# Element-wise two-tensor operations of more than 300 elements on VectorE alone, small ones also on GpSimd, in a two-layer attention encoder

## The chip, the cores and the metric

One core of a Trainium2 chip runs the whole program. The metric is device time in microseconds of one execution: the median of several runs, and beside it the time of one profiled execution, on which the trace is made. Engines are named as in the profile: PE (matrix products), DVE (VectorE), ACT (ScalarE), POOL (GpSimd), SP (issues DMA).

## What is computed

Two sequences, of 1024 and of 512 positions, go through the same two encoder layers; 16 learned positions are put ahead of each, so that the kernel works on 1040 + 528 = 1568 columns of width 1024. Everything is in 32-bit floats. Cut to what matters:

```python
def layer(x, cos, sin, w_in, w_out, pre_g, post_g, sink, lq1, lk1, lq2, lk2, subln_g, lambda_init):
    h = rmsnorm(x, pre_g)
    aq, ak, av, ag, bq, bk, bv, bg = split(einsum('bld,de->ble', h, w_in))
    aq, ak = apply_rope(aq, cos, sin), apply_rope(ak, cos, sin)
    oa = window_gqa_attention(aq, ak, av, sink) * silu(ag)      # 8 heads, a window of 128 on either side
    lam = exp(sum(lq1 * lk1)) - exp(sum(lq2 * lk2)) + lambda_init
    bq, bk = apply_rope(bq, cos, sin), apply_rope(bk, cos, sin)
    ob = diff_attention(bq, bk, bv, lam, lambda_init, subln_g) * silu(bg)   # softmax(c=0) - lam * softmax(c=1)
    o = einsum('ble,ed->bld', concatenate([oa, ob]), w_out)
    return x + rmsnorm(o, post_g)
```

## The kernel before

Features lie on the partitions, positions along the free dimension. The 1568 columns are worked on in four chunks of 392 (`CH`). For each layer the program has these steps: `prestats` and `rstd_bc` sum the squares of a chunk and broadcast the reciprocal root `rb` of it; `prenorm` scales the chunk; `load_w` brings weights; `inproj` and `project` multiply and make queries, keys, values and gates (with rope), which are stored to HBM; `attn_b` (four heads of the differential kind) and `attn_a` (two groups of the windowed kind) read them back; `outproj` multiplies by `w_out`, and its `post` normalises, adds the residual and stores.

A product is made in two parts for precision: every operand is split into a rounded part `hi` and the rest `lo = x - hi`, and three products are summed in PSUM (`dense`: hi by hi, hi by lo, lo by hi). So each weight tile (`whl`, 128x1024), each normalised chunk (`slot`), each rope result (`st`) and each probability tile (`at`) needs a copy and then a subtraction. `dense` writes its sums to `ps_d`, which has two buffers; `ps_s` holds scores, `ps_t` transposes, `ps_o` attention outputs.

Nothing is issued in the order of the code. `Recorder` notes each operation with what it reads and writes, its priority, and a cost for each engine that can do it (`Engine.form`, lines 460 to 522). `schedule` (line 323) then runs through time by these costs and hands the next ready operation of highest priority to an engine that is free; an operation that has two engines goes to whichever can take it first. What comes out is one fixed order for each engine, which `emit` issues (line 445, the line that all instructions carry in the profile). Each engine then works its own queue in that order and waits at its head.

Operations with two engines come from three helpers: `any_copy` (ACT or DVE), the squares of `prestats` in the first layer (ACT or POOL, line 722), and `any_tt` (line 296, DVE or POOL), which is called for all two-tensor additions, subtractions and products whose inputs both lie in SBUF:

```python
            cost = 0.15 + n * (0.0022 if name == "tensor_tensor" else 0.0035)   # POOL, line 512
                cost = 0.066 + n * 0.001042                                      # DVE, line 508
```

`n` is the number of elements per partition. Both forms also carry a mark `port`; by it the planner lets no two of them overlap in time (lines 398 to 408).

Names of tiles: `t` (in the code `t1`) holds the first half of a rope product or the running sum of squares of an output chunk; `ru` and `rw` are rope products or squares; `sm` small columns (minima, sums, reciprocal roots); `pp` probabilities; `og` attention output; `pad` the last 16 keys. In `rstd_bc` POOL always does two short operations on `sm` (TENSOR_SCALAR, and a power with `mhalf`), between two transposes of PE.

Of the kernel before, what the change touches and what calls it, by code (L numbers as in the profile page):

```python
# [125 lines left out]
ENG = ("PE", "ACT", "DVE", "POOL", "SP")  # L126
PE_COL = 0.0004453
PE_SWITCH = 0.39


def _size(pat, shape, kw):
# [106 lines left out]
class Recorder:  # L238
# [55 lines left out]
        return self.call([g[0] for g in got], got[0][1], got[0][2])  # L294

    def any_tt(self, out, a, b, op):
        return self.any((self.vector, "tensor_tensor", (out, a, b), dict(op=op)),
                        (self.gpsimd, "tensor_tensor", (out, a, b), dict(op=op)))

# [158 lines left out]
class Engine:  # L458
# [3 lines left out]
    def form(self, name, args, kw):  # L462
# [14 lines left out]
        elif self.eng == "PE":  # L477
# [10 lines left out]
            if src.shape[0] <= 64:  # L488
                cost += PE_SWITCH
        elif self.eng == "ACT":  # L490
# [1027 lines left out]
```

## Time and profile before

| | before |
|---|---|
| median of 3 runs (lowest, highest) | 1985.34 us (1983.41, 1994.87) |
| the profiled execution | 1988.96 us |
| its span from the first to the last instruction | 1986.8 us |
| mean granted clock of PE | 0.972 |
| busy: PE, DVE, ACT, POOL | 1841.9, 1509.0, 1015.0, 825.2 us |

The profiled execution is 0.2% above the median. The span leaves 2.2 us of it outside. A stretch in which PE is busy throughout is at PE's pace, whatever the other engines do; the waits of PE in the other stretches say whose result ended last.

### The profile page before, as it was taken

The page shows a single profiled execution, that of the slowest core. Times are in us where ns is not written, and L with a number is a line of the kernel's source. Part 1 is how long each engine was busy: PE and PEld are TensorE (multiplying, and loading weights), DVE is VectorE, ACT ScalarE, POOL GpSimd, SP SyncE. Part 2 cuts the span into 40 slices and gives each one's busy share as a digit, 9 for nine tenths or more (in the row PEclk, how much of TensorE's full clock was granted, in tenths as well). Part 3 has the DMA queues.
Part 4 walks back from the last instruction along what each step waited for, and adds up shares of the span by engine and source line. Part 5 has one row for each costly group of instructions (what it writes and reads, how often), then busy time and mean ns, then how long its engine had stood idle before and what let it go on. Part 6 is the DMA issues. An engine that isn't in the chain of part 4 may idle for free. (4 is left out here: it accounts for less than half of the span.)

```text
span 1986.8 us, 33503 instructions
## 1 busy us (share of the span) xinstructions
PE 1841.9 (93%) x11424; PEld 1757.3 (88%) x11424; DVE 1509.0 (76%) x3043; ACT 1015.0 (51%) x2358; POOL 825.2 (42%) x833
## 2 busy tenths in 40 slices
PE   5899999999999998999966999999999999899995
PEld 4889989989999988998856999999999998899994
DVE  7858777787777797687986577777877859768768
ACT  3325445454544575576544355555545537547541
POOL 6634362352352351002788452452613513421157
PEclk8999999999999999999978999999999999999997
DMA  6253363443434665555442535445453464764453
GB/s 229 60 159 112 104 169 100 135 128 111 141 93 122 165 176 158 120 134 144 158 151 84 151 98 152 128 128 158 115 173 96 124 166 120 193 176 102 122 173 130
DMA packets 289012, 271.06 MB, mean 136 GB/s; under 512 B 91402, under 2 KB 266058, under 8 KB 288714
## 3 DMA queue, kind: packets, MB, share of 16 engines
q1 hardware_dynamic: 288842, 268.92, 48.1%
q8 instruction: 91, 1.49, 0.3%
q14 instruction: 79, 0.65, 0.1%
HBM read 147.43 MB, written 95.94 MB: 122 GB/s over the span
## 5 line engine op out<-in xcount | busy, mean ns | idle before, releaser
L445 PE MATMUL ps_d<-slot,whl 128*128 128x392 f32 (+2 forms) x5712 | 1180.6, 349 | 53.6 <-POOL slot L445 13.7
L445 PEld LDWEIGHTS ps_d<-slot,whl 128*128 128x128 f32 x5712 | 998.5, 191 | 71.1 <-POOL slot L445 17.1
L445 PE MATMUL ps_s<-kk,qq 128*128 128x264 f32 (+9 forms) x1496 | 286.0, 318 | 18.0 <-DMA BS<-st 4.1
L445 PE MATMUL ps_o<-at,vv 128*128 128x256 f32 (+6 forms) x1368 | 286.3, 308 | 11.1 <-DVE at L445 5.5
L445 DVE TENSOR_TENSOR at<-ps_t,at 128x256 fp32r<-128x256 f32 (+6 forms) x472 | 224.7, 480 | 75.1 <-ACT at L445 67.8
L445 ACT ACTIVATE pp<-ps_s,sm 116x1040 f32<-116x1040 f32 (+4 forms) x208 | 203.9, 980 | 149.2 <-DVE sm L445 138.6
L445 ACT ACTIVATE at<-ps_t 128x256 fp32r<-128x256 f32 (+12 forms) x430 | 183.1, 434 | 166.8 <-PE ps_t L445 153.2
L445 PEld LDWEIGHTS ps_s<-kk,qq 128*128 128x128 f32 (+4 forms) x1496 | 229.1, 184 | 42.0 <-issue 5.2
L445 DVE TENSOR_REDUCE sm<-ps_s 116x1 f32<-116x1040 f32 (+4 forms) x208 | 218.7, 1051 | 51.5 <-PE ps_s L445 48.6
L445 ACT ACTIVATE pp<-pp,sm 128x336 f32<-128x336 f32 (+5 forms) x339 | 201.2, 606 | 77.3 <-DVE sm L445 74.9
L445 PEld LDWEIGHTS ps_o<-at,vv 128*128 128x128 f32 (+1 forms) x1368 | 215.0, 189 | 21.0 <-DVE at L445 9.2
L445 PE MATMUL ps_t<-ident,pp 128*128 128x128 f32 (+4 forms) x1208 | 196.4, 271 | 4.3 <-DVE pp L445 3.1
L445 PEld LDWEIGHTS ps_t<-ident,pp 128*128 128x128 f32 (+4 forms) x1208 | 143.6, 137 | 18.2 <-DVE pp L445 2.9
L445 POOL TENSOR_TENSOR sm<-sm 128x2 f32<-128x2 f32 (+2 forms) x112 | 49.6, 443 | 263.7 <-DVE sm L445 263.1
L445 POOL TENSOR_TENSOR pad<-pp,pad 128x64 fp32r<-128x64 f32 (+5 forms) x121 | 36.2, 302 | 231.3 <-DVE pad L445 117.2
L445 POOL TENSOR_TENSOR pp<-pp 128x1040 f32<-128x1040 f32 (+4 forms) x36 | 75.1, 2085 | 125.3 <-ACT pp L445 125.2
L445 POOL TENSOR_TENSOR whl<-wraw,whl 128x1024 fp32r<-128x1024 f32 x40 | 97.6, 2440 | 64.6 <-ACT whl L445 31.7
L445 POOL TENSOR_TENSOR slot<-slot 128x784 f32<-128x784 f32 (+7 forms) x41 | 93.6, 2286 | 39.3 <-ACT slot L445 14.4
L445 DVE CUSTOM_DVE_ANT_0 pp<-ps_s,mk,nsinks 128x336 f32<-128x336 f32 (+2 forms) x192 | 97.5, 525 | 16.1 <-PE ps_s L445 15.0
L445 POOL TENSOR_TENSOR ru<-ru,rw 128x392 f32<-128x392 f32 (+1 forms) x60 | 66.5, 1112 | 58.4 <-DVE rw L445 47.2
L445 ACT ACTIVATE og<-ps_o 64x128 f32<-64x128 f32 (+4 forms) x248 | 66.0, 287 | 47.6 <-PE ps_o L445 30.4
L445 DVE CAST at<-ps_t 128x256 fp32r<-128x256 f32 (+10 forms) x138 | 70.2, 509 | 16.6 <-PE ps_t L445 12.8
(157 smaller groups left out, 2442.1 us busy)
## 6 DMA issues: line engine op xcount, KB each, us to landing
wraw<-in_w_in_dram SPq DMA_DIRECT2D x48, 512.0 KB
BS<-st SPq DMA_DIRECT2D x112, 196.0 KB
qq<-qq SPq DMA_DIRECT2D x144, 128.0 KB
qq<-AQ SPq DMA_DIRECT2D x96, 128.0 KB
BV<-st SPq DMA_DIRECT2D x28, 392.0 KB
wraw<-in_w_out_dram SPq DMA_DIRECT2D x20, 512.0 KB
slot<-in_x_dram SPq DMA_DIRECT2D x12, 784.0 KB
GT<-ru SPq DMA_DIRECT2D x48, 196.0 KB
```

What stands on the lines that cost most here:

```text
L445: fn(*[_real(a) for a in args], **{k: _real(a) for k, a in kw.items()})
```

## The change

`any_tt` asks for the size of its output per partition. Over 300 elements the operation is recorded for DVE alone; at 300 or fewer it can go to DVE or POOL as before. No other line changes. The planner then makes new orders for all five queues.

```diff
--- before.py
+++ after.py
@@ -126,6 +126,7 @@
 ENG = ("PE", "ACT", "DVE", "POOL", "SP")
 PE_COL = 0.0004453
 PE_SWITCH = 0.39
+POOL_MAX = 300
 
 
 def _size(pat, shape, kw):
@@ -294,6 +295,11 @@
         return self.call([g[0] for g in got], got[0][1], got[0][2])
 
     def any_tt(self, out, a, b, op):
+        n = 1
+        for k in out.shape[1:]:
+            n *= k
+        if n > POOL_MAX:
+            return self.vector.tensor_tensor(out, a, b, op=op)
         return self.any((self.vector, "tensor_tensor", (out, a, b), dict(op=op)),
                         (self.gpsimd, "tensor_tensor", (out, a, b), dict(op=op)))
```

At the start of the program, on DVE, from the squares of the first chunk to the first reduction for a reciprocal root (`slot` sums of squares and split chunks, `rw` a rope product). Before:

```order
L445 TENSOR_TENSOR slot<-slot 128x784
L445 SCALAR_TENSOR_TENSOR slot<-slot,preg 128x392
L445 TENSOR_TENSOR slot<-slot 128x784 x2
L445 TENSOR_TENSOR slot<-slot 128x392
L445 SCALAR_TENSOR_TENSOR rw<-ps_d,scl,cs 128x392 x2
L445 TENSOR_TENSOR slot<-slot 128x784
L445 TENSOR_REDUCE sm<-ps_t 98x4
L445 TENSOR_TENSOR slot<-slot 128x784
L445 TENSOR_TENSOR slot<-slot 128x2x376
L445 TENSOR_TENSOR slot<-slot 128x392
```

After:

```order
L451 TENSOR_TENSOR slot<-slot 128x784
L451 TENSOR_TENSOR whl<-pp,whl 128x1024
L451 TENSOR_TENSOR slot<-slot 128x784
L451 SCALAR_TENSOR_TENSOR slot<-slot,preg 128x392
L451 TENSOR_TENSOR slot<-slot 128x392
L451 TENSOR_TENSOR slot<-slot 128x784
L451 TENSOR_TENSOR kk<-pp,kk 128x1024
L451 TENSOR_REDUCE sm<-ps_t 98x4
L451 TENSOR_TENSOR vv<-pp,vv 128x1024
L451 TENSOR_TENSOR slot<-slot 128x784
L451 TENSOR_SCALAR subg<-subg 128x1
```

The subtractions for three weight tiles (`whl`, `kk`, `vv`, 128x1024) now stand among the sums. They came from POOL's queue, which was, from the first squares to the first chain on `sm`:

```order
L445 TENSOR_TENSOR slot<-slot 128x784 x3
L445 TENSOR_TENSOR whl<-pp,whl 128x1024
L445 TENSOR_TENSOR kk<-pp,kk 128x1024
L445 TENSOR_TENSOR vv<-pp,vv 128x1024
L445 TENSOR_TENSOR slot<-slot 128x2x376 x2
L445 TENSOR_SCALAR sm<-sm 98x4
```

and is now:

```order
L451 TENSOR_TENSOR slot<-slot 128x784 x3
L451 TENSOR_SCALAR sm<-sm 98x4
L451 TENSOR_TENSOR sm<-sm,mhalf 98x4
L451 TENSOR_TENSOR slot<-slot 128x2x376 x2
L451 TENSOR_SCALAR sm<-sm 98x4
```

The chain on `sm` stands ahead of the squares of the next chunk.

Where layer 0 ends and layer 1 begins, on POOL (`slot` the residual sums, the sums of squares and the split chunks; `at` a chunk being normalised; `kk`, `vv` weights). Before, from one chain on `sm` to the next:

```order
L445 TENSOR_SCALAR sm<-sm 98x4
L445 TENSOR_TENSOR kk<-wraw,kk 128x1024
L445 TENSOR_TENSOR sm<-sm,mhalf 98x4
L445 TENSOR_TENSOR slot<-slot 128x784
L445 TENSOR_TENSOR slot<-at,slot 128x392
L445 TENSOR_TENSOR slot<-slot 128x784
L445 TENSOR_TENSOR at<-at,rb 128x392
L445 TENSOR_TENSOR slot<-slot 128x784
L445 TENSOR_TENSOR vv<-wraw,vv 128x1024
L445 TENSOR_TENSOR slot<-slot 128x784
L445 TENSOR_TENSOR at<-at,rb 128x392
L445 TENSOR_SCALAR sm<-sm 98x4
```

After:

```order
L451 TENSOR_TENSOR pad<-pp,pad 128x2x32 x2
L451 TENSOR_SCALAR sm<-sm 98x4
L451 TENSOR_TENSOR sm<-sm,mhalf 98x4
L451 TENSOR_TENSOR og<-og,gl 128x256
L451 TENSOR_SCALAR sm<-sm 98x4
```

POOL holds only chains on `sm` there, and products on `og` and `pad` of the attention that ends. On DVE, in the same stretch of the program, from one reduction for a chain to the next, before:

```order
L445 TENSOR_REDUCE sm<-ps_t 98x4
L445 TENSOR_TENSOR at<-at,rb 128x392
L445 SCALAR_TENSOR_TENSOR slot<-slot,postg,rb 128x392 x7
L445 COPY rb<-ps_t 128x392
L445 SCALAR_TENSOR_TENSOR slot<-slot,postg,rb 128x392
L445 TENSOR_TENSOR t_11573<-t_11573,ru 128x392
L445 TENSOR_TENSOR slot<-at,slot 128x392
L445 TENSOR_REDUCE sm<-ps_t 98x4
```

After:

```order
L451 TENSOR_REDUCE sm<-ps_t 98x4
L451 TENSOR_TENSOR vv<-wraw,vv 128x1024
L451 SCALAR_TENSOR_TENSOR rw<-ps_d,scl,cs 128x392
L451 TENSOR_TENSOR ru<-t_12002,cs 128x392 x2
L451 SCALAR_TENSOR_TENSOR rw<-ps_d,scl,cs 128x392
L451 TENSOR_TENSOR ru<-ru,rw 128x392 x2
L451 TENSOR_TENSOR slot<-slot 128x1568
L451 SCALAR_TENSOR_TENSOR slot<-slot,postg,rb 128x392
L451 TENSOR_TENSOR slot<-slot 128x784
L451 SCALAR_TENSOR_TENSOR slot<-slot,postg,rb 128x392
L451 TENSOR_TENSOR slot<-slot 128x392
```

The split of a weight tile (`vv`), rope products (`ru`) and sums of squares (`slot`, 128x784) that POOL did stand between DVE's own scalings now.

At the end of the program, from the last reduction on, DVE before:

```order
L445 TENSOR_REDUCE sm<-ps_t 128x3
L445 TENSOR_TENSOR slot<-slot,rb 128x384 x2
L445 TENSOR_TENSOR slot<-slot 128x384 x2
L445 SCALAR_TENSOR_TENSOR slot<-slot,postg,rb 128x384 x4
L445 TENSOR_TENSOR slot<-slot 128x384
```

POOL before:

```order
L445 TENSOR_SCALAR sm<-sm 128x3
L445 TENSOR_TENSOR sm<-sm,mhalf 128x3
L445 TENSOR_TENSOR slot<-slot,rb 128x384 x2
L445 TENSOR_TENSOR slot<-slot 128x384 x5
```

DVE after (POOL has nothing behind its last chain on `sm`):

```order
L451 TENSOR_REDUCE sm<-ps_t 128x3
L451 TENSOR_TENSOR slot<-slot,rb 128x384 x4
L451 TENSOR_TENSOR slot<-slot 128x384 x4
L451 SCALAR_TENSOR_TENSOR slot<-slot,postg,rb 128x384 x4
L451 TENSOR_TENSOR slot<-slot 128x384 x4
```

Two products with `rb` and five additions have moved from POOL to DVE.

## Rows read from the trace of the kernel before

**Rows 1.** The page: busy us of each engine (share of span) x instructions.
```profile
PE 1841.9 (93%) x11424; PEld 1757.3 (88%) x11424; DVE 1509.0 (76%) x3043; ACT 1015.0 (51%) x2358; POOL 825.2 (42%) x833
```

**Rows 2.** Stretches: length, busy PE, PEld, DVE, ACT, POOL (x instructions), PEclk, DMA, GB/s.
```profile
0.00:100.00 100.00, 72.18 (x376) 67.11 (x377) 78.37 (x108) 38.60 (x65) 62.75 (x50) 0.93 0.46 145
100.00:940.00 840.00, 805.69 (x5114) 771.06 (x5113) 630.52 (x1396) 444.00 (x1077) 282.21 (x346) 0.99 0.49 134
940.00:1110.00 170.00, 129.25 (x656) 116.78 (x655) 141.54 (x158) 81.96 (x143) 144.47 (x99) 0.87 0.38 123
1110.00:1900.00 790.00, 773.02 (x4944) 744.97 (x4944) 590.28 (x1306) 427.46 (x1031) 281.44 (x299) 1.00 0.51 141
1900.00:1987.00 87.00, 61.72 (x340) 57.41 (x339) 68.26 (x77) 22.94 (x44) 54.34 (x41) 0.88 0.40 133
```

**Rows 3.** Waits of PE, 940 to 1110 us: us in total, times, longest.
```profile
PE ps_d L445 <- POOL slot L445: 12.2, 7, 3.3
PE ps_t L445 <- POOL sm L445: 7.9, 3, 7.3
PE ps_d L445 <- DVE slot L445: 7.6, 7, 2.7
PE ps_t L445 <- DVE t L445: 5.6, 1, 5.6
```

**Rows 4.** Timeline of DVE, 985 to 1105 us: start, duration, operation, xcount.
```profile
1020.75 12.48 DVE L445 SCALAR_TENSOR_TENSOR slot<-slot,postg,rb 128x392 f32<-128x392 f32 x7 [0.30 <-ACT rb L445]
...
1053.47 4.37 DVE L445 SCALAR_TENSOR_TENSOR slot<-slot,postg,rb 128x392 f32<-128x392 f32 x8
```

**Rows 5.** Timeline of POOL, the same stretch.
```profile
1053.64 5.21 POOL L445 TENSOR_SCALAR sm<-sm 98x4 f32<-98x4 f32 x1 [1.52 <-DVE sm L445]
```

**Rows 6.** Groups of POOL by shape: xcount, busy us, mean ns, idle before.
```profile
L445 POOL TENSOR_TENSOR whl<-wraw,whl 128x1024 fp32r<-128x1024 f32 x40 | 97.6, 2440 | 64.6 <-ACT whl L445 31.7 <-DVE whl L445 29.0 <-DVE sm L445 3.3
L445 POOL TENSOR_TENSOR ru<-ru,rw 128x392 f32<-128x392 f32 x50 | 54.5, 1096 | 47.4 <-DVE rw L445 36.3 <-DVE ru L445 6.5 <-DVE sm L445 3.7
```

**Rows 7.** Groups of DVE by shape.
```profile
L445 DVE SCALAR_TENSOR_TENSOR slot<-slot,postg,rb 128x392 f32<-128x392 f32 x32 | 37.5, 1222 | 0.3 <-ACT rb L445 0.3
...
L445 DVE TENSOR_TENSOR ru<-ru,rw 128x392 f32<-128x392 f32 x30 | 28.7, 955 | 0.5
```

**Rows 8.** Stretches, the whole span, of instructions on tile sm alone.
```profile
0.00:1987.00 1987.00, 28.31 (x164) 20.51 (x164) 457.80 (x997) 444.28 (x1003) 142.54 (x256) 0.97 0.48 136
```

**Rows 9.** Waits of PE, first 100 us.
```profile
PE ps_t L445 <- POOL sm L445: 5.5, 2, 4.3
PE ps_t L445 <- DVE ru L445: 3.5, 1, 3.5
...
PE ps_d L445 <- POOL whl L445: 1.9, 1, 1.9
```

**Rows 10.** Waits of PE, 1900 us to the end.
```profile
PE ps_t L445 <- POOL t L445: 4.6, 1, 4.6
```

**Rows 11.** Waits of PE, 100 to 940 us.
```profile
PE ps_o L445 <- DVE at L445: 3.9, 6, 2.7
PE ps_t L445 <- DVE pp L445: 3.1, 4, 1.1
```

**Rows 12.** Waits of PE, 1110 to 1900 us.
```profile
PE ps_d L445 <- DVE ru L445: 6.5, 3, 4.2
PE ps_d L445 <- DVE rw L445: 3.2, 1, 3.2
```

**Rows 13.** Timeline of DVE, 1969 us to the end.
```profile
1973.87 1.82 DVE L445 TENSOR_TENSOR slot<-slot,rb 128x384 f32<-128x384 f32 x2 [2.74 <-ACT rb L445]
...
1982.58 1.23 DVE L445 TENSOR_TENSOR slot<-slot 128x384 f32<-128x384 f32 x1
```

**Rows 14.** Waits of all engines, whole span.
```profile
ACT pp L445 <- DVE sm L445: 213.6, 204, 10.1
...
POOL pp L445 <- ACT pp L445: 125.2, 32, 9.0
```

## The prediction

> **What bounds the kernel now.** I began with the page's first block: PE is busy 93% of the span, DVE 76%, ACT 51%, POOL 42% [rows 1]. Nothing but PE can be the bound over the whole program, so a change on DVE and POOL pays only where PE stands still. The table of stretches says where that is [rows 2]. In the two long stretches (100 to 940 us, and 1110 to 1900 us) PE is busy 805.7 of 840 and 773.0 of 790 us, at a granted clock of 0.99 and 1.00. In the three short ones, which I call the borders, it isn't: 72.2 of the first 100 us, 129.3 of the 170 us in which layer 0 ends and layer 1 begins, 61.7 of the last 87; and the clock is 0.93, 0.87 and 0.88. So 94 us of PE's idle time lie in 357 us of borders, 51 us in the other 1630.
>
> Then I asked who ends PE's waits. In the middle border these are POOL (12.2 us on `slot`, 7.9 on `sm`) and DVE (7.6 and 5.6) [rows 3]. In the first 100 us POOL's `sm` and `whl` stand beside DVE's `ru` (5.5, 1.9, 3.5) [rows 9], at the end POOL's accumulator `t` (4.6) [rows 10]. In the long stretches POOL is not among the large ones: the two largest of each are DVE's, 3.9 + 3.1 + 6.5 + 3.2 = 16.7 us [rows 11, 12]. I expect a gain, if there is one, in the borders, and a loss, if there is one, in the long stretches.
>
> **How DVE and POOL get in each other's way.** One view settles this [rows 4]. At 1020.75 seven independent SCALAR_TENSOR_TENSOR of 128x392 take 12.48 us on DVE (1.78 each) while POOL runs adds; at 1053.47 eight of the same take 4.37 us (0.55 each) while POOL runs none. The same kind of work costs three times as much beside POOL. In the other direction POOL's TENSOR_SCALAR on 98x4 elements takes 5.21 us from 1053.64, until those eight and the two behind them are through [rows 5]. Operations of the two engines that read two SBUF tensors do not run side by side here: POOL is no second pair of hands for this kind of work, only a slower one.
>
> **The change part by part.**
>
> *What moves.* Counted in the built programs, two-input operations of over 300 elements go from 383 on DVE and 375 on POOL to 753 and 6; POOL keeps the small `sm`, `pad` and `og` ones, and the squares that don't go through the changed function. So 370 instructions move. The two largest groups of them have 90 instructions in 152.1 us, 1.69 us each [rows 6]; widths from 376 to 1568 stand beside them, so I take 1.65: 610 us leave POOL. The bound from above is 825.2 [rows 1] less 142.5 on `sm` [rows 8], 683; from below 370 x 1.10, 405.
>
> *What they cost on DVE.* A 392-wide operation costs 1096 ns on POOL [rows 6] and 0.55 us on undisturbed DVE [rows 4], so one half: 305 us, between 200 and 340.
>
> *What DVE gets back.* Its own two-input operations stop waiting for POOL's long ones. Two groups show 1222 and 955 ns on average [rows 7] where 0.55 is the undisturbed price: (0.67 x 32 + 0.40 x 30) / 62 = 0.54 us each. Over the 383 that is at most 205 us; groups that meet POOL less often will have perhaps 0.3, 115 us. I take 170.
>
> *DVE's sum.* 1509 + 305 - 170 = 1644 us, 83% of the span, with 1560 to 1730 as the bounds (1509 + 250 - 200 and 1509 + 340 - 115). This is the number on which I rest most: DVE takes over 610 us of POOL's work for some 135 us more of its own time, and stays below PE.
>
> *The middle border.* In the seven operations of 12.48 us, 7 x 0.55 = 3.9 are DVE's own and 8.6 are POOL's; these cost half on DVE, so the stretch takes 8.2, a third less. All the waits named in [rows 3], 33.3 us, are on such mixed stretches. A third of it is 11 us. If only POOL's `slot` wait is shortened by half it is 6; if nothing else is behind it, 20.
>
> *The first 100 us.* Waits of 5.5, 3.5 and 1.9 [rows 9], a third: 4 us (0 to 6). The order of DVE shows the split of the weights moved in ahead of sums of squares, so part of it is only exchanged.
>
> *The end.* After the last broadcast, DVE and POOL multiply, add and scale from 1973.87 to 1983.81, 9.9 us [rows 13]. In the new order these are 16 operations in a row on DVE, at 0.53 us 8.5 us: 1.4 less. Of the 4.6 us for POOL's accumulator [rows 10] I take a third. Together 3 us (1 to 5).
>
> *The long stretches.* Here POOL's work lay beside DVE's reads of PSUM, and the cover goes. DVE is busy 1220.8 of 1630 us now [rows 2], idle 25%; with 9% more work (1644 / 1509) it is idle 18%. If PE's waits for it grow as its idle share falls, by 25/18, 16.7 us become 23: 6 us lost (0 to 12). ACT has half its time free and gets six instructions more, so I cost that at nothing. SP issues the same transfers; no queue but DVE's, POOL's and ACT's has other work in it.
>
> *Sum.* Against the profiled execution's own time: 1989.0 - 11 - 4 - 3 + 6 = 1977. That execution lies 3.6 us above the median of the runs, so the median should be about **1973 us**, 0.6% less than before. Each term at its bounds gives 1946 to 1990 from the borders and the waiting of the long stretches.
>
> **A rule against the trace.** POOL keeps the short chain that turns a sum of squares into a reciprocal root: TENSOR_SCALAR and a power, sixteen times in the borders. The row shows that DVE's unbroken run kept such an operation out for 5.2 us [rows 5]. The Trainium skill, "SBUF — State Buffer", section "Who interferes with whom", says that whoever issues first gets the shared pair for the whole instruction and the other is fully blocked; by that, POOL would wait for one DVE instruction at most (0.55 us here), and sixteen chains could lose 9 us in all. The trace doesn't agree: POOL waited through ten, and by the row sixteen chains could lose 83. The sum above does not include this, because runs of the same kind stand behind these chains before the change also; it is the third rival.
>
> **The rivals.**
>
> *Border gains are larger.* If the waits named for the borders, 33.3 + 10.9 + 4.6 = 48.8 us, halve (24), and PE's clock in the middle one comes back from 0.87 to 0.95 for its 129 us of work (10 us), the time is 1989 - 34 - 2 (end) = 1953 less 3.6: about 1950. For it: both engines named there are the two that block each other. Against: the order moves, and what PE waits for next in those places is ACT and DMA.
>
> *DVE's queue becomes the bound: slower.* POOL waited 125.2 us for ACT's scaled `pp` alone [rows 14], and nobody stood behind it but POOL's own work. In DVE's queue the same operation holds up the reads of PSUM behind it, and PE has two `ps_d` buffers. If PE's waits for DVE in the long stretches become four times as long, 16.7 to 67, the time is 1989 + 50 - 10 = 2029 less 3.6, 2025. It decides from the point where DVE, busy and held up together, fills over some nine tenths of a long stretch; with 82% busy that needs 130 us of holding up, half a microsecond for each of the some 250 moved operations that stand there (POOL has 282 and 281 of its 825 us in these stretches [rows 2]). For it: ACT already waits 213.6 us for DVE's minima of the scores [rows 14]. Against: each is planned where its input is due, and before the change DVE's own `whl` and `pp` operations were held up less than that. The Trainium skill, "Perfetto Trace Analysis", section "Optimizing Scalar/DVE Operations", would move work off a saturated DVE, even to GPSIMD, and adds that the shared port may make it useless; at 76% [rows 1] the first half does not apply yet.
>
> *POOL's short chains starve.* With only DVE work in the borders, runs without a gap are longer. If each of the sixteen waits 2 us more, the time is 1973 + 32 = 2005. For it: [rows 5]. Against: in DVE's order the runs behind these reductions add up to about the same.
>
> *Nothing changes.* DVE's busy time in the borders stays what it was, since it takes half of POOL's work and loses its own waiting; if it was the chain there, the borders stay as long: 1985 to 1990.
>
> **How the numbers follow.** About 1% (20 us) is what a measurement of this kernel can tell from no change. Forecast (1962 to 1984): 0.40. Larger gains in the borders: 0.20. Nothing changes: 0.17. DVE's queue: 0.15. Starving chains: 0.08. Faster by over 1% (below 1965.5) holds the larger gains and a quarter of the forecast: 0.30. Slower by over 1% (above 2005) holds DVE's queue, half of the starving chains and a little for mishaps of the order: 0.21. Within 1%: 0.49. The range reaches into the larger gains and to where DVE's queue begins to decide: 1948 to 2015. The likeliest case's own range is 1962 to 1984.
>
> **What would show it.** DVE busy 1560 to 1730 us and POOL about 200. 128x392 two-input operations on DVE near 0.55 us on average, and no group of them over 0.8. PE's busy share in 940 to 1110 us up from 129 of 170, and its waits for POOL there gone but for `sm`. PE's waits for DVE in the long stretches below 25 us. I am wrong if those waits exceed 50 us, if POOL's TENSOR_SCALAR of 98x4 takes over 2 us on average, or if DVE's busy time goes above 1750.

## The result, and the profile after

The changed kernel takes 1967.03 us (median of 4 runs, 1960.32 to 1970.75) against 1987.88 for the kernel before: a ratio of 0.9888, with a 95% interval of 0.9847 to 0.993. That is 21 us or 1.1% less, just past the 1% that a measurement here can tell from no change. I had forecast 1973 (1962 to 1984 for the likeliest case, 1948 to 2015 in all). The time is inside both, but not by the sum that led there: three of its four terms came out outside their own ranges, and the gain is 21 us where the sum had 12.

The first block of the page of the changed kernel, which answers to [rows 1] (busy us of each engine, share of the span, instructions):

```profile
PE 1839.0 (94%) x11424; PEld 1751.8 (89%) x11424; DVE 1551.5 (79%) x3384; ACT 1013.2 (52%) x2364; POOL 272.8 (14%) x486
```

POOL gave up 552 us, and DVE needs only 42 us more for them (1509.0 before). The groups of DVE by shape say why; beside [rows 7] they read now (xcount, busy us, mean ns):

```profile
L451 DVE TENSOR_TENSOR ru<-ru,rw 128x392 f32<-128x392 f32 x80 | 42.9, 556 | 0.0
L451 DVE SCALAR_TENSOR_TENSOR slot<-slot,postg,rb 128x392 f32<-128x392 f32 x32 | 19.0, 631 | 2.7 <-ACT rb L451 2.7
```

955 ns has become 556, and 1222 has become 631: little holds DVE's own operations up any more. One group of this width is still slow, eight `slot<-slot,preg` of the first 20 us at 923 ns on average: two of them take 1.86 us, while POOL still works on sums of squares. The price stands in a group of POOL, TENSOR_SCALAR of 98x4 elements, before and after:

```profile
L445 POOL TENSOR_SCALAR sm<-sm 98x4 f32<-98x4 f32 x11 | 10.7, 973 | 7.6 <-DVE sm L445 7.0
L451 POOL TENSOR_SCALAR sm<-sm 98x4 f32<-98x4 f32 x11 | 19.6, 1780 | 109.0 <-DVE sm L451 109.0
```

Its mean has gone from 973 to 1780 ns. An undisturbed one takes 0.19 us (a row of the last experiment shows one).

**Where PE's time went.** Fixed times, as in [rows 2], cut two plans at different work. So I cut both programs at the same four points: where DVE begins to read the 20th, the 140th, the 160th and the 260th tile of attention scores. Columns are those of [rows 2]: stretch, length, busy PE (x instructions), PEld, DVE, ACT, POOL, granted clock, DMA share, GB/s. The kernel before:

```profile
0.00:223.29 223.29, 191.15 (x1109) 182.93 (x1110) 161.34 (x246) 89.60 (x162) 102.86 (x92) 0.95 0.47 139
223.29:903.45 680.16, 650.94 (x4162) 621.38 (x4161) 514.74 (x1161) 366.29 (x902) 229.86 (x290) 0.99 0.50 134
903.45:1198.69 295.24, 252.60 (x1412) 235.62 (x1411) 230.75 (x347) 146.41 (x290) 194.37 (x150) 0.92 0.42 130
1198.69:1772.84 574.15, 558.87 (x3609) 540.51 (x3608) 432.46 (x915) 300.93 (x712) 213.30 (x230) 0.99 0.52 144
1772.84:1987.00 214.16, 188.29 (x1140) 176.90 (x1139) 169.68 (x378) 111.73 (x293) 84.81 (x71) 0.95 0.45 133
```

The changed kernel:

```profile
0.00:215.02 215.02, 192.22 (x1124) 184.25 (x1125) 164.03 (x291) 91.27 (x164) 35.28 (x49) 0.97 0.49 145
215.02:898.26 683.24, 657.78 (x4218) 626.84 (x4217) 547.98 (x1255) 360.89 (x903) 104.70 (x211) 0.99 0.50 134
898.26:1169.04 270.78, 230.88 (x1283) 215.92 (x1283) 223.29 (x429) 139.28 (x282) 42.54 (x48) 0.91 0.43 132
1169.04:1752.64 583.60, 570.04 (x3664) 547.56 (x3663) 449.56 (x994) 307.11 (x720) 73.93 (x153) 1.00 0.52 143
1752.64:1964.50 211.86, 188.10 (x1143) 177.23 (x1141) 166.68 (x422) 114.64 (x297) 16.38 (x25) 0.96 0.46 136
```

Length less busy PE is PE's idle time. Here it is for every kernel of this study, worked out in this way from its own stretches (the plan of before was profiled twice, that of the changed kernel three times; these are means):

| PE idle, us | start | first long | middle | second long | end | all |
|---|---|---|---|---|---|---|
| before (2) | 31.4 | 29.6 | 42.6 | 15.3 | 25.8 | 144.8 |
| changed (3) | 22.9 | 25.3 | 41.5 | 14.6 | 23.7 | 128.0 |
| before's plan, large operations on DVE | 33.4 | 34.9 | 31.2 | 24.8 | 25.7 | 149.8 |
| norms and output projection on DVE | 27.0 | 31.3 | 44.6 | 11.8 | 24.4 | 139.0 |
| projections, weights, attention on DVE | 27.3 | 29.0 | 54.2 | 15.3 | 27.9 | 153.8 |
| changed, chains by Newton steps on DVE | 23.5 | 27.6 | 49.3 | 15.8 | 26.4 | 142.7 |
| changed, reduction done twice | 23.4 | 25.6 | 43.5 | 16.4 | 24.3 | 133.2 |
| before, another plan | 30.0 | 35.9 | 57.4 | 12.5 | 35.2 | 170.9 |
| changed, another plan | 23.6 | 27.2 | 35.8 | 15.2 | 25.5 | 127.2 |

Executions of one plan come close in it: 145.1 and 144.4 before, 125.5, 130.7 and 127.8 after. PE's busy time moves more (1841.9 and 1850.7 us in the two executions of before; 1839.0, 1838.1 and 1837.7 after). The spans of these five executions differ by 24.7 us on average: 17 are waiting that PE no longer does, 8 are busy time, which I can't tell from its scatter with two executions of before. Half of the 17 lies at the start, not in the middle border where I had put most of it. The middle stretch is 24 us shorter, but 22 of these are PE's own work that the new plan does elsewhere: 1283 matrix products stand there instead of 1412, and the stretches around it have 15, 56 and 55 more.

The waits of PE from 940 to 1110 us, where [rows 3] stood (us in total, times, longest):

```profile
PE ps_t L451 <- POOL sm L451: 21.4, 5, 10.5
PE ps_d L451 <- DVE slot L451: 9.8, 7, 3.7
PE ps_d L451 <- DVE rw L451: 1.2, 2, 0.7
```

POOL's `slot` (12.2) and DVE's `t` (5.6) are gone as forecast. In their place POOL's `sm`, the short chain of the norms, went from 7.9 to 21.4.

### The profile page after: what moved, and what is told of

It reads as the page before. It is cut to its first block, busy times and chain, and to the rows that moved or that the text cites. A ratio compares the mean times of both kernels' runs of the same rounds, so it can differ in the third digit from the quotient of the medians.

```text
span 1964.5 us, 33387 instructions
## 1 busy us (share of the span) xinstructions
PE 1839.0 (94%) x11424; PEld 1751.8 (89%) x11424; DVE 1551.5 (79%) x3384; ACT 1013.2 (52%) x2364; POOL 272.8 (14%) x486
## 5 line engine op out<-in xcount | busy, mean ns | idle before, releaser
L451 PE MATMUL ps_d<-slot,whl 128*128 128x392 f32 (+2 forms) x5712 | 1176.7, 348 | 29.7 <-DVE slot L451 15.4
L451 PE MATMUL ps_o<-at,vv 128*128 128x256 f32 (+6 forms) x1368 | 286.6, 308 | 11.3 <-DVE og L451 4.3
L451 ACT ACTIVATE at<-ps_t 128x256 fp32r<-128x256 f32 (+9 forms) x435 | 187.8, 440 | 178.4 <-PE ps_t L451 167.3
L451 POOL TENSOR_TENSOR pad<-pp,pad 128x64 fp32r<-128x64 f32 (+3 forms) x143 | 47.2, 332 | 790.9 <-ACT pad L451 487.4
L451 POOL TENSOR_TENSOR sm<-sm 128x2 f32<-128x2 f32 (+3 forms) x112 | 53.1, 475 | 477.9 <-DVE sm L451 464.4
L451 DVE CUSTOM_DVE_ANT_0 pp<-ps_s,mk,nsinks 128x336 f32<-128x336 f32 (+2 forms) x192 | 97.8, 526 | 17.1 <-PE ps_s L451 15.4
L451 DVE TENSOR_TENSOR slot<-slot 128x784 f32<-128x784 f32 (+8 forms) x74 | 83.7, 1146 | 7.3 <-ACT slot L451 7.0
L451 DVE TENSOR_TENSOR whl<-wraw,whl 128x1024 fp32r<-128x1024 f32 x62 | 76.5, 1234 | 5.4 <-ACT whl L451 5.0
L451 POOL TENSOR_SCALAR sm<-sm 128x2 f32<-128x2 f32 (+6 forms) x72 | 51.8, 720 | 190.7 <-DVE sm L451 185.8
L451 ACT ACTIVATE pad<-pp 128x64 fp32r<-128x64 f32 (+5 forms) x144 | 33.4, 236 | 82.8 <-DVE pp L451 79.2
L451 ACT ACTIVATE ru<-ps_d 128x392 f32<-128x392 f32 (+3 forms) x93 | 45.6, 490 | 57.6 <-PE ps_d L451 49.3
## 6 DMA issues: line engine op xcount, KB each, us to landing
qq<-qq SPq DMA_DIRECT2D x144, 128.0 KB
qq<-AQ SPq DMA_DIRECT2D x96, 128.0 KB
```

Of the source, the lines that this page charges most:

```text
L451: fn(*[_real(a) for a in args], **{k: _real(a) for k, a in kw.items()})
```

## The experiments

**Is it a draw?** The changed kernel once more, beside the three kernels that follow.

> The changed kernel once more, beside three kernels that split the change. If its gain is real and not a draw of four runs, it stays 0.7 to 1.4% below the kernel before (ratio 0.986 to 0.993). If it was a draw, the interval reaches 1.

1970.67 us against 1990.98, a ratio of 0.9892 (0.9872 to 0.9911). It is no draw of the runs; whether it is one of the plans is a question of its own, asked below.

**The same plan, other engines.** The plan of before is kept; only when the operations are issued, a large one that was planned for POOL goes to DVE.

```diff
     def any_tt(self, out, a, b, op):
-        return self.any((self.vector, "tensor_tensor", (out, a, b), dict(op=op)),
-                        (self.gpsimd, "tensor_tensor", (out, a, b), dict(op=op)))
+        o = self.any((self.vector, "tensor_tensor", (out, a, b), dict(op=op)),
+                     (self.gpsimd, "tensor_tensor", (out, a, b), dict(op=op)))
+        if out.shape[1:] and np.prod(out.shape[1:]) > 300:
+            o.repl = o.alts["DVE"][1]
+        return o
...
-            for fn, args, kw in o.calls:
+            for fn, args, kw in getattr(o, 'repl', o.calls):
```

> The plan of the kernel before, untouched, with the large two-input operations that it gives to POOL handed to DVE at the same places in the order. Contention theory (the gain is POOL's long operations no longer standing in DVE's way): DVE's busy time falls to about 1550 us as in the changed kernel and most of the gain is kept, 1965 to 1978 us. Order theory (the gain comes from the new plan, which moves work into and out of the borders): DVE's busy time falls just the same, but the time stays at 1983 us or more, since operations stand in DVE's queue where POOL's slower pace wanted them.

2009.96 us, a ratio of 1.0099 (1.0079 to 1.0119): 1% slower than before, on the side of the order theory and further than it had said, though DVE's busy time is 1565.6 us as the contention theory wanted. The table shows two terms of my sum at work. PE's idle time in the middle falls by 11.4 us, the 11 of the forecast. In the two long stretches it rises by 5.3 and 9.5. The waits of PE from 1110 to 1890 us say for whom:

```profile
PE ps_o L448 <- DVE at L448: 8.6, 17, 1.4
PE ps_d L448 <- DVE ru L448: 8.1, 3, 4.7
PE ps_s L448 <- DVE sm L448: 3.9, 3, 2.6
```

`at` are the probabilities that DVE brings from PSUM for the next product; I read the seventeen short waits as DVE's queue, in which these reads now stand behind operations that used to lie on POOL. All rows of PE's waits for DVE between 100 and 940 and between 1110 and 1900 us add up to 46.6 us, against 27.6 before and 20.4 in the changed kernel. At the start PE's idle time rises by 2.0 us and at the end it stays, so what the changed kernel gains there isn't in the change of engine. The idle time as a whole grows by 5 us only; most of the 19 us stands in PE's busy time, 1855.0 us against 1841.9 and 1850.7 before. It grew in the products that take `at` (groups of PE: xcount, busy us, mean ns, idle before), before and here:

```profile
L445 PE MATMUL ps_o<-at,vv 128*128 128x256 f32 (+6 forms) x1368 | 286.3, 308 | 11.1 <-DVE at L445 5.5 <-ACT at L445 2.4 <-DVE og L445 2.4
L448 PE MATMUL ps_o<-at,vv 128*128 128x256 f32 (+6 forms) x1368 | 297.6, 311 | 31.4 <-DVE at L448 17.9 <-DVE og L448 9.6 <-ACT at L448 2.7
```

The same products are 11 us longer busy (286.4 in the other execution of before, 286.6 in the changed kernel), besides the 20 us more of idle time ahead of them. So the change of engine alone is a loss here, and the gain needs the new plan. That the new plan gains by setting the moved operations where they don't stand ahead of PSUM reads is my reading of these waits; no run tests it by itself.

**One half at a time.** `dve_tt` has the new rule and `any_tt` the old one. First kernel: `dve_tt` in `prestats`, `scaled`, `prenorm`, `squares`, `load_mix` and `post`. Second kernel: in all other places.

```diff
+    def dve_tt(self, out, a, b, op):
+        if np.prod(out.shape[1:]) > 300:
+            return self.vector.tensor_tensor(out, a, b, op=op)
+        return self.any_tt(out, a, b, op)
...
-                nc.any_tt(acc[:, 0:n], acc[:, 0:n], sq[:, 0:n], ALU.add)
+                nc.dve_tt(acc[:, 0:n], acc[:, 0:n], sq[:, 0:n], ALU.add)
```

> Only the two-input operations of the norms and the output projection (sums of squares, scaling, the norm's split, the residual's add, the split of the mixed rows) are held to DVE, the others are planned freely as before. Border theory: nearly the whole gain, 1963 to 1975 us, with the middle border about 25 us shorter as in the changed kernel. Rival (the gain needs POOL quiet everywhere): at most a third of it, 1980 us or more.

> The other half: only the two-input operations of the projections, the split of weights and the attention are held to DVE; those of norms and output projection are planned freely. Border theory: little, 1980 to 1990 us, because PE hardly waited for these in the long stretches. Rival (the split of weights on POOL is what PE waits for): 1970 us or less.

The first takes 1987.06 us (ratio 0.9987, 0.9971 to 1.0003), the second 2005.39 (1.0074, 1.0055 to 1.0093). Neither half brings the gain, against the border theory; the first agrees with its rival. The second fits neither of its two expectations: it is slower than before. Both would fit contention that stays while POOL has large operations left (POOL is busy 641.6 and 499.2 us in them), but that is argued. In the first, PE's idle time falls by 4.4 us at the start (8.5 with the whole change) and by 3.5 in the second long stretch, and grows by 2 each in the first long one and the middle. But each kernel has a plan of its own, and the next pair shows how much that alone can do. So I don't read the 16 and 35 us between them and the changed kernel as the price of the halves, and the border theory isn't settled by this pair.

**How much is the plan?** The planner adds a random offset of up to 5 places to each priority; the work and the rule for the engines are the same.

```diff
-SPREAD = 0
+SPREAD = 5
```

> The kernel before, planned with a random offset of up to 5 places on each operation's priority: the same work on the same engines by the same rule, in a slightly different order. With the two kernels below it tells how much of a per cent is the luck of one plan. If the change's gain is its own, this one stays within 5 us of 1991 and its changed counterpart 15 to 25 us below it. If plans scatter, this one lies 10 us or more from 1991 by itself, and the pairs differ by amounts that range over 20 us.

> The changed kernel, planned with the same random offsets. Own gain: 15 to 25 us below the kernel before with those offsets. Scatter: the difference of this pair is anything from 10 us more to 40 us less.

Before, with this plan: 2021.41 us (1.0154, 1.014 to 1.0168), 30 us more than with its own. Changed, with this plan: 1972.76 (0.9907, 0.989 to 0.9924), 2 us more. One pair of plans differs by 20 us and the other by 49. The sign is the same in both; the size depends on which plan of before is taken, and the other plan of before moved the time by 30 us, more than the change did. In the stretch in the middle (same columns as above), before and changed, with these plans:

```profile
919.07:1213.07 294.01, 236.64 (x1300) 217.65 (x1300) 238.78 (x332) 141.30 (x278) 192.94 (x145) 0.89 0.40 121
896.06:1172.90 276.84, 241.03 (x1337) 225.77 (x1336) 226.57 (x440) 139.29 (x281) 44.79 (x48) 0.92 0.43 131
```

With about as many matrix products there (1300 and 1337), PE is idle 57.4 us in the one and 35.8 in the other.

A third pair was meant to add another plan:

```diff
-PE_SWITCH = 0.39
+PE_SWITCH = 0.4
```

> A third plan of the kernel before: the planner's cost of a change of PE's row group is 0.40 instead of 0.39, nothing else. If the plan of the kernel before lies low among its neighbours (the second lay at 2021), this one is at 2000 to 2025 us. If the second was an outlier, 1985 to 1995.

> A third plan of the changed kernel, with the same 0.40. If the change's own gain is larger than what the two given plans show, this one is again within 10 us of 1971, and 25 us or more below its counterpart. If plans scatter on this side too, anything from 1960 to 2000.

1991.17 and 1970.7 us. But the edit changed no row of any engine's order, in either kernel: these are repeats of the two given plans, 0.9995 (0.998 to 1.0011) and 0.9904 (0.9883 to 0.9926), and say nothing on other plans. With two plans on each side, it stays open how far plans scatter, and so how much of the 21 us belongs to the rule and how much to this pair of plans.

**Does POOL's short chain cost what PE waits for it?** In the changed kernel's own order, each norm's chain is issued on DVE, with the power replaced by Newton steps (each improves an estimate of the reciprocal root by three short operations). The plan still has POOL's two operations; `repl` is what is issued in their place.

```diff
-            nc.gpsimd.tensor_scalar(col[0:m, ja:jb], col[0:m, ja:jb], scale, EPS, op0=ALU.mult, op1=ALU.add)
-            nc.gpsimd.tensor_tensor(col[0:m, ja:jb], col[0:m, ja:jb], mhalf[0:m, ja:jb], op=ALU.pow)
...
+            nc.last.repl = [
+                (dv.tensor_scalar, (z, c, -0.5 * scale, -0.5 * EPS), dict(op0=ALU.mult, op1=ALU.add)),
+                (dv.tensor_scalar, (c, z, seed ** 3, 1.5 * seed), dict(op0=ALU.mult, op1=ALU.add))]
+            for _ in range(4 if seed == 3.0 else 2):
+                nc.last.repl += [
+                    (dv.tensor_tensor, (w, c, c), dict(op=ALU.mult)),
+                    (dv.tensor_tensor, (w, w, z), dict(op=ALU.mult)),
+                    (dv.scalar_tensor_tensor, (c, w, 1.5, c), dict(op0=ALU.add, op1=ALU.mult))]
+            nc.gpsimd.tensor_tensor(c, c, mhalf[0:m, ja:jb], op=ALU.pow)
+            nc.last.repl = []
...
```

> The changed kernel in its own order, with the short chains of the norms (scale, power) computed on DVE by Newton steps from a constant start that holds for the means of squares of these inputs alone. PE waited 21.4 us for POOL's sm in the middle border and 5.8 in the first 100 us. If these waits come from POOL being kept out behind DVE's runs, they fall below 8 us together and the time by 10 to 18 us, to 1953 to 1961. If PE would have waited for DVE there anyway, POOL's waits turn into waits for DVE and the time stays within 5 us of 1970.

1983.55 us (0.9955, 0.9941 to 0.9969): 13 us slower than the changed kernel, the waits turned up for DVE, as the second theory had it, and cost more than its 5 us. Its first block, and its waits of PE from 940 to 1110 us:

```profile
PE 1839.5 (93%) x11424; PEld 1751.0 (88%) x11424; DVE 1578.6 (80%) x3560; ACT 1014.8 (51%) x2364; POOL 229.8 (12%) x454
...
PE ps_d L451 <- DVE slot L451: 22.5, 13, 6.2
PE ps_t L451 <- DVE sm L451: 15.4, 3, 11.7
```

With no POOL in the chain PE still waits 15.4 us for `sm`, 11.7 of it in one piece (10.5 with POOL), and more than twice as long for `slot`. DVE has 26 us more work (1578.6 against 1552.2 in the repeat) and the time is 13 us longer. This alone doesn't price POOL's lateness, since the Newton steps make the chain itself longer. The trace of the changed kernel does. Around PE's longest wait for `sm`, rows of PE (the sums go to `ps_t`; the result of the chain comes back), of DVE and of POOL:

```profile
950.34 0.60 PE L451 MATMUL ps_t<-ident,t 128*98 128x128 f32 x4
...
964.11 0.91 PE L451 MATMUL ps_t<-ident,sm 98*128 98x98 f32 x4 [10.50 <-POOL sm L451]
```

```profile
961.36 0.69 DVE L451 TENSOR_REDUCE sm<-ps_t 98x4 f32<-98x512 f32 x1
```

```profile
962.14 0.44 POOL L451 TENSOR_SCALAR sm<-sm 98x4 f32<-98x4 f32 x1 [4.62 <-DVE sm L451]
962.66 1.40 POOL L451 TENSOR_TENSOR sm<-sm,mhalf 98x4 f32<-98x4 f32 x1
```

The sums lie in PSUM at 950.94, and DVE reduces them at 961.36: for 10.4 us the reduction stands in DVE's queue, behind scalings and sums that DVE does without a gap. POOL's two operations then take 0.6 us more than the shortest of their kind (0.19 and 1.01). Ahead of the other four waits for `sm` (1.7, 3.1, 4.7 and 1.4 us) they take 2.0, 4.5, 2.3 and 2.2 us more. No wait can hold more of POOL's lateness than the shorter of its two numbers, and these add up to 9 us. So at least 12 of the 21.4 us that the waits put down to POOL's `sm` aren't POOL being kept out. No run moved the reduction forward in DVE's queue.

**The exclusion by itself.** A kernel apart from the program, which leaves the computation out: a reduction on DVE releases POOL's TENSOR_SCALAR of 98x4, and behind the reduction DVE has a run of independent operations of 128x392.

```python
for n in (0, 4, 8, 16, 32):
    behind(n, "tt")        # reduction, n two-input operations on DVE; TENSOR_SCALAR on POOL
```

> A kernel of its own that measures the exclusion alone and leaves the whole computation out. Thirteen stages, each fenced: a reduction on DVE, then a run of independent DVE operations of 128x392 behind it, and POOL's TENSOR_SCALAR of 98x4 that the reduction releases; runs of 0, 4, 8, 16 and 32 two-input operations, then of 16 with one operand in PSUM, 16 of one input, 16 SCALAR_TENSOR_TENSOR; then POOL and DVE with a run each. Starvation theory: POOL's operation lasts as long as the run, about 2.2, 4.4, 8 and 17 us for 4, 8, 16 and 32, and 0.2 us behind the PSUM run. By the Trainium skill, page SBUF — State Buffer, section Who interferes with whom, it would wait for one DVE instruction, under 1 us behind each run.

The starvation theory fell in this form. POOL's timeline (start, duration, operation, xcount) behind 4, 16 and 32 two-input operations, then behind 16 that read one operand from PSUM:

```profile
6.33 0.44 POOL L69 TENSOR_SCALAR colb<-colb 98x4 f32<-98x4 f32 x1 [1.07 <-DVE colb L65]
...
15.01 0.45 POOL L69 TENSOR_SCALAR cold<-cold 98x4 f32<-98x4 f32 x1 [5.10 <-DVE cold L65]
25.35 0.45 POOL L69 TENSOR_SCALAR cole<-cole 98x4 f32<-98x4 f32 x1 [9.90 <-DVE cole L65]
...
56.62 0.20 POOL L69 TENSOR_SCALAR colg<-colg 98x4 f32<-98x4 f32 x1 [10.83 <-DVE colg L65]
```

0.45 us whatever the run, a quarter of a microsecond more than undisturbed. But DVE's operations here all wrote the same tile, and 16 of them took 9.56 us, 0.60 each, where in the kernel one starts every 0.48 us and lasts 0.56, so that it overlaps the next. The second kernel writes eight tiles in turn.

```diff
-            o = cp.tile([128, 392], F32, name=name("o"))
-            for _ in range(n):
...
+            outs = [cp.tile([128, 392], F32, name=name("o") + str(i)) for i in range(min(n, 8))]
+            for i in range(n):
+                o = outs[i % 8]
...
```

> The measuring kernel again (it leaves the whole computation out), but DVE's run writes to eight tiles in turn, so that its operations overlap as they do in the kernel (a start every 0.48 us, each 0.56 long), where in the first one all wrote to one tile and started every 0.60 us. Theory: what keeps POOL out is that DVE's two-input operations overlap without a gap; then POOL's TENSOR_SCALAR lasts as long as the run again, 2, 4, 8 and 15 us behind 4, 8, 16 and 32, and 0.4 us behind the run that writes one tile. Rival: POOL gets in after one DVE operation whatever the run, 0.4 to 0.5 us in every stage as in the first; then the 4 to 5 us seen in the two kernels have another cause.

The timeline of POOL behind 4, 8, 16 and 32; then (`colf`) behind 16 SCALAR_TENSOR_TENSOR; `colg`, behind 16 that write one tile; `colh`, behind 16 that read PSUM; `coli`, `colj`, behind eight two-input operations that alternate with eight reads of PSUM and with eight copies:

```profile
6.33 1.87 POOL L70 TENSOR_SCALAR colb<-colb 98x4 f32<-98x4 f32 x1 [1.07 <-DVE colb L66]
9.27 3.78 POOL L70 TENSOR_SCALAR colc<-colc 98x4 f32<-98x4 f32 x1 [1.07 <-DVE colc L66]
14.12 7.60 POOL L70 TENSOR_SCALAR cold<-cold 98x4 f32<-98x4 f32 x1 [1.07 <-DVE cold L66]
22.80 15.23 POOL L70 TENSOR_SCALAR cole<-cole 98x4 f32<-98x4 f32 x1 [1.07 <-DVE cole L66]
39.09 8.56 POOL L70 TENSOR_SCALAR colf<-colf 98x4 f32<-98x4 f32 x1 [1.07 <-DVE colf L66]
48.73 0.44 POOL L70 TENSOR_SCALAR colg<-colg 98x4 f32<-98x4 f32 x1 [1.07 <-DVE colg L66]
59.07 0.19 POOL L70 TENSOR_SCALAR colh<-colh 98x4 f32<-98x4 f32 x1 [9.90 <-DVE colh L66]
67.50 0.44 POOL L70 TENSOR_SCALAR coli<-coli 98x4 f32<-98x4 f32 x1 [8.23 <-DVE coli L66]
75.95 5.97 POOL L70 TENSOR_SCALAR colj<-colj 98x4 f32<-98x4 f32 x1 [8.01 <-DVE colj L66]
```

In all these rows the run keeps POOL out to its end if its operations overlap and none reads PSUM: 15.23 us for an operation of 0.19. A gap, or an operation that reads PSUM, lets it in; copies in between do not (5.97). So [rows 5] can happen by such a run alone. But one later stage of this kernel goes the other way. POOL's operation is released by a copy there and has a run of its own behind it; DVE's run of 16 begins first. Behind two-input operations (`tl`) POOL is kept out as before, behind SCALAR_TENSOR_TENSOR (`tm`) it gets in after the first one. POOL's two rows, then DVE's run beside `tm`:

```profile
92.26 7.59 POOL L82 TENSOR_SCALAR tl<-tl 128x4 f32<-128x4 f32 x1 [0.56 <-DVE tl L79]
...
108.13 0.49 POOL L82 TENSOR_SCALAR tm<-tm 128x4 f32<-128x4 f32 x1 [0.56 <-DVE tm L79]
```

```profile
107.95 14.74 DVE L57 SCALAR_TENSOR_TENSOR om<-ga,tok,gb 128x392 f32<-128x392 f32 x16
```

The first two operations of `tm`'s run overlap too (starts at 107.95 and 108.49, each 0.62 long), and the same operations kept POOL out for 8.56 us in `colf`. So overlap isn't the whole condition; what else decides stays open. The page "SBUF — State Buffer" of the Trainium skill, section "Who interferes with whom", gives the shared pair to one instruction at a time; the runs agree with that where DVE's operations don't overlap (0.44 us) and in `tm` (0.49), and not in the other runs whose operations overlap.

**Letting POOL in.** If an operation that reads PSUM opens the way, a second reduction behind the first should do, at 0.6 us of DVE for each chain instead of the Newton steps.

```diff
...
+            nc.last.repl = nc.last.alts["DVE"][1] + [(real.vector.tensor_reduce, (), dict(
+                out=gap[0:m, 4 * (pass_[0] % 4) + ja:4 * (pass_[0] % 4) + jb],
+                in_=pt[0:m, 128 * ja:128 * jb].rearrange("p (j e) -> p j e", e=128), axis=AX, op=ALU.add))]
```

> The changed kernel in its own order, with the reduction of each norm's chain done twice on DVE (the second result goes unused): 0.6 us of DVE work that reads PSUM alone, behind which POOL's TENSOR_SCALAR should get in, as it did behind the runs that read PSUM. First, POOL's TENSOR_SCALAR of 98x4 should fall from 1780 ns on average to 500 or less. Starvation theory (what PE loses to sm in the middle border is POOL being kept out): PE's wait for sm there falls from 21.4 to below 13 us and the time by 5 to 10 us, to 1961 to 1966. Rival (DVE's throughput decides in the borders, the moved wait turns up for DVE): sixteen times 0.6 us, 10 us more on DVE, cost what 26 us cost with the Newton steps (13 us) by proportion: 1971 to 1977 us, with PE's waits for DVE there longer by what those for sm lose.

1975.02 us (0.9914, 0.9901 to 0.9928): 4 us above the changed kernel (0.9892, 0.9872 to 0.9911), a difference that the two intervals don't clear. It lies in the range of the rival, and no gain of 5 to 10 us shows. But the edit didn't do its first job: POOL's TENSOR_SCALAR of 98x4 takes longer than the 1780 ns without it. Its group, then two places that show why, in DVE's timeline and in POOL's:

```profile
L451 POOL TENSOR_SCALAR sm<-sm 98x4 f32<-98x4 f32 x11 | 25.5, 2316 | 103.3 <-DVE sm L451 103.3
```

```profile
945.92 0.68 DVE L451 TENSOR_REDUCE gap<-ps_t 98x4 f32<-98x512 f32 x1
946.51 0.27 DVE L451 SCALAR_TENSOR_TENSOR og<-ps_o,og 64x128 f32<-64x128 f32 x1
...
1007.40 0.68 DVE L451 TENSOR_REDUCE gap<-ps_t 98x4 f32<-98x512 f32 x1
1008.00 1.03 DVE L451 TENSOR_TENSOR slot<-at,slot 128x392 fp32r<-128x392 f32 x2
```

```profile
946.09 0.19 POOL L451 TENSOR_SCALAR sm<-sm 98x4 f32<-98x4 f32 x1 [0.40 <-DVE sm L451]
...
1007.57 5.31 POOL L451 TENSOR_SCALAR sm<-sm 98x4 f32<-98x4 f32 x1 [8.95 <-DVE sm L451]
```

Both times POOL asks while the second reduction still has half a microsecond to go. At 946.09, with a PSUM read behind it, POOL is through in 0.19 us. At 1007.57, with a two-input operation behind it, it is kept out during the reduction too, until the run ends 5.3 us later. Of all eleven, ten take 0.50 to 0.60 us longer than in the changed kernel, and the second reduction moves the run behind it by 0.60. So here the exclusion reaches back to before the two-input operation starts; how far, these runs don't tell. The Trainium skill, in the section just named of "SBUF — State Buffer", lists this reduction among the operations that never contend; at 946.09 it doesn't, and at 1007.57 what stands behind it does. What it would cost PE if POOL got in at once stays untested.

## Why the prediction held, and where it didn't

**PE is the bound, and DVE's and POOL's times count only where PE waits.** Right: PE's share of the span went from 93% to 94%.

**DVE's sum, 1644 us (1560 to 1730).** Too high: 1551.5, just under its range. The lower end was itself mis-added: I had put the moved operations at 200 to 340 and then used 250. Contention given back was the right size. Over every DVE group by shape, the durations less count times the shortest of its kind come to 235 us before and 55 after, so 180 where I had 170. The operations moved cost less than 305: the sum of DVE's durations grew by 83 us, and 83 + 180 is 263. And I had not thought of overlap: operations in an unbroken run start every 0.48 us and last 0.56, which busy time counts once; that takes the growth from 83 to 42.

**POOL about 200 us.** It is 272.8. The 610 us that were to leave were right: POOL's operations of over 300 elements took 609.5 us before and take 11.1. What I had not priced is that the small ones grow, `sm` from 142.5 [rows 8] to 164 and `pad` and `og` by 18 together, and I had left out 23 us of rope products of up to 256 columns.

**The middle border, 11 us (6 to 20).** This step failed, though its mechanism did not. With the plan held still the 11 us are there (31.2 us of PE's idle time against 42.6). In the new plan they aren't (41.5). It has 129 fewer matrix products in that stretch to cover the same chain of norms, which may be why; the count alone doesn't decide it, since the two half kernels have 1353 and 1359 there and idle 44.6 and 54.2 us. I had costed the change in the old order, with the new order at hand.

**The first 100 us, 4 us (0 to 6).** 8.5 up to the 20th score tile, twice as much and outside the range. With the order held still this stretch got 2.0 us more idle time, so the term's mechanism isn't what gave the gain; the new order is. PE's waits there [rows 9] fell for POOL (9.6 to 5.8 us in all), DVE (6.9 to 3.8) and ACT (11.2 to 8.4).

**The end, 3 us (1 to 5).** 2.1, and 0.1 with the order held still. The sixteen operations behind the last broadcast take 7.8 us where [rows 13] had 9.9 and I had worked out 8.5.

**The long stretches, a loss of 6 us (0 to 12).** Wrong in sign for the changed kernel: PE's waits for DVE fell from 27.6 to 20.4 us and its idle time by 5. Right in sign and too small for the old plan: there the idle time grew by 15. The base of the term was too small as well: I had counted the largest rows, 16.7 us. I had taken DVE's load as what counts; the waits look as if it were which operations stand ahead of its PSUM reads. The bound of 25 us for those waits held.

**The rivals.** DVE's queue as the bound is real but needs the old plan: 2010 us there. Starving chains came true in part: POOL's operation grew by 0.8 us on average (973 to 1780 ns), not by 2, and at least 12 of PE's 21.4 us in the middle aren't theirs. Larger border gains and no change didn't come; the granted clock in the middle, which the former wanted back, stayed at 0.92 and 0.91. Against the rule of one DVE instruction I had set [rows 5] as a counterexample; the second kernel on the exclusion bears this out, and the first, with `tm` of the second, shows why the rule can look right.

**The sum.** It was 12 us and PE's idle time fell by 17, but -8.5, -5, -1 and -2 stand where I had -4, +6, -11 and -3 (start, long stretches, middle, end): errors of 16 us one way and 11 the other offset each other. That the time fell into the range is partly luck. The range of the sum was also mis-added: the terms at their bounds give 1954 to 1990, not 1946.

## What to carry to other kernels

Price a move from one engine to another with the order held still and once more in the order that the planner makes; here the first was 19 us slower and the second 21 faster. Before trusting a difference of one per cent between two planned kernels, plan both again with a small offset: one plan of the same kernel was 30 us off. And POOL was mostly kept waiting here not by one operation of DVE but by a whole unbroken run, so short steps of a critical chain fit it badly where such runs stand.

## What the hardware showed that I had not expected

Whether POOL is kept out for a whole run depends on whether DVE's operations overlap: 7.60 us behind 16 that write eight tiles, 0.44 behind 16 that write one. One overlapping run, `tm`, let it in all the same.

Where POOL is in, the two take turns, and both lose. In the second kernel on the exclusion, 16 operations of DVE and 8 of POOL ran against each other, started so that POOL's came first; DVE's timeline, then POOL's:

```profile
124.23 13.45 DVE L53 TENSOR_TENSOR on<-ga,gb 128x392 f32<-128x392 f32 x16
```

```profile
123.28 10.16 POOL L96 TENSOR_TENSOR qn<-ga,gb 128x392 f32<-128x392 f32 x8
```

While POOL's eight last, both engines start one operation about every 1.3 us; DVE's other eight follow at 0.48. POOL's take 1.27 us each instead of 0.97 (7.77 us for eight alone in this kernel). The same turns follow `tm`, where DVE was first. [rows 4] looks like this state, [rows 5] like the other one of the same pair.

More work on DVE for the norms' chains cost the whole about half of itself: 26 us of Newton steps cost 13. The second reduction's 8.5 us and 4.4 would fit, but that difference isn't clear of noise, and in both the chain itself is longer.
